# Prompt attention with full-row key products and one value group for each query block

## The chip, the cores and the metric

The kernel runs on one core of one Trainium2 chip. The metric is the device time of one execution in microseconds. Three runs of the kernel before took 994.25, 989.42 and 985.31 us; their median is 989.42 us.

## What is computed

The reference is one inference step of a decoder layer for 512 prompt tokens and 8 sampled sequences of 4 tokens each (544 columns in all, width 1024). One normalised input is projected once; three mixers take their parts of it, and a merge and an output projection end the step. The part around which the change lies is the prompt's attention: 8 query heads in 2 groups of 4, head size 64, with a compressed, a selected and a window branch. For 512 prompt tokens the selected and the window branch see all earlier keys.

```python
h = rmsnorm(x, norm_g) @ w_in                     # one projection, columns split over the mixers
# attention, for each group g, head r of the group, query block of 128
p_c = masked_softmax(q . kcmp + bias)             # 31 compressed keys
p_s = masked_softmax(q . k_sel + bias, causal)    # branch 1
p_w = masked_softmax(q . k_win + bias, causal)    # branch 2
o   = gate0 * p_c @ vcmp + gate1 * p_s @ v_sel + gate2 * p_w @ v_win
# mLSTM (4 heads x 128, chunks) and gated DeltaNet (4 heads x 128, 8 chunks of 64, state S)
o_g: A = tril(kb k^T) ; u, w = (I + A)^-1 [v b, kb e^G] ; S <- S e^GL + k^T (u - w S)
# merge: x + sum_i(sigmoid(merge_i) * ((o_i * silu(z_i)) @ w_branch_i)) @ w_out
```

All of it is float32 to the reference's accuracy, so that a product of two operands is made from an upper and a lower part of each (`wh`, `wl`, `xh`, `xl`): three products instead of one.

## The kernel before

**Order of the work.** The program is traced in Python and a scheduler then writes, for each engine, one fixed list of instructions, by priority and by the times that it expects. Most of TensorE's work are projections: `gemm_steps` (L400 to L410, the products are L407) makes a tile of 128 outputs from 24 products for each half of the 544 tokens, 128x272 each. Tiles of the mixers' gates and of the merge wait in `queue`; `low()` and `fill(n)` (L584 to L599) put them in the list at a low priority, so that they stand between the steps of a chain that has to wait. Each tile of weights is loaded by the SP queue (L390), split by ScalarE (L393) and by VectorE or GpSimd (L396). All engines, and the SP queue's loads and stores too, run their lists in order.

**Places.** Nearly all buffers are ranges of one big tile, `arena`; `Reg(n)` hands out the first free range of n columns, `free()` gives it back, and two further tiles are lent to it while their places are free (`low2`, `low3`). A range that is handed out again waits for the last reader of what lay there.

**Prompt attention** (`att`, L1261 to L1304; head r = 0 is traced ahead of the mLSTM, heads 1 to 3 after it). For a head of both groups, it walks through 4 query blocks i of 128; w = 128 (i + 1) keys are in reach. For each branch b and group g: the scores are an upper product over 128 rows (L1278: both parts of the query against the key's upper part) and a lower product over 64 rows (L1280: the query's upper part against the key's lower part), 128 x w. VectorE adds the bias and takes the maximum (L1285), ScalarE the exponential (L1288), VectorE normalises and gates (L1290), TensorE transposes in pieces of 128 (L351), VectorE or ScalarE copy to a ring `ptr2`. The value products (L1300) add into `acc`, group 0 to its rows 0 to 63 and group 1 to 64 to 127: output tiles of 64 columns of the array. The compressed branch's product comes first (L1272), over 32 rows. The lower parts of the keys of both groups share one slot of `kst`, group 0 on rows 0 to 63 and group 1 on rows 64 to 127 (L1216).

**DeltaNet.** The samples' part loads 8 states of 4 heads (L1570, `Sg`, 4096 columns), forms their outputs (L1597 to L1624), updates them in 8 steps (product L1629, VectorE L1632) and stores them in two halves (L1633). The prompt's part builds decay tables (L1673: `Dm`, `bb`), `Db`, the matrix B (L1689, L1691), inverts its blocks through DRAM (L1712 store, L1714 eight loads back, L1724 and L1726 a chain of small steps on VectorE, L1728 stores, L1729 load back, L1731), composes the inverse (L1742) and then walks through 8 chunks: products L1774, L1785, L1792, L1805 with VectorE and ScalarE between them (L1777, L1787, L1799). A head norm follows chunks 3 and 7 (L1312 to L1316, transposes L351). Then come merge and output, with L1899 and L407.

Of the kernel before, what the change touches and what calls it, by code (L numbers as in the profile page):

```python
# [32 lines left out]
AC = 24932  # L33
A1 = 1280
A2 = 3072
# [55 lines left out]
def _consts():  # L91
# [26 lines left out]
    # one row for each norm, in each group of 32: row t * 2 + g is column 14 of a slice that starts at 14 - 2 t  # L118
# [54 lines left out]
def _layout(i):  # L173
# [33 lines left out]
    # (position of a pair, feature), (tap, pair of positions), group  # L207
# [36 lines left out]
def tile_step(ctx: ExitStack, tc: tile.TileContext, A, O):  # L244
# [20 lines left out]
    # two more tiles, while their places are free: columns 0 to A1 and A1 + 1 to A1 + 1 + A2, the arena's after those  # L265
# [13 lines left out]
    class Reg:  # L279
        """A range of the arena's columns, handed out from its start."""  # L280
# [118 lines left out]
    def gemm_steps(wt, mh, ml, k, sink, rot=0):  # L399
        # the two halves of the tokens, in steps of 8 products  # L400
# [31 lines left out]
    # products of zeros raise the tensor engine's clock while x comes  # L432
# [36 lines left out]
    def norm(k):  # L469
        # the split of the normalised x, for all later projections  # L470
# [6 lines left out]
    # page ids: a row for the registers, and rows of the pools seen as [page, 8 blocks, NQ] for the indirect loads  # L477
# [25 lines left out]
    # gates of the samples' rows (b, g, t, r), two sets of four samples  # L503
# [34 lines left out]
    def silu2(j):  # L538
        # twice silu of a projected tile
# [30 lines left out]
    # outputs of the three branches, feature-major  # L570
# [4 lines left out]
    def prime():  # L575
        # the next tile, its weights on their way
        if queue:
            name, f, t = queue.pop(0)
            g = f(t)
            next(g)  # L580
            job.append((name, g))

    def fill(n):
        # steps of projections that wait for nothing, put between the steps of a chain  # L584
# [8 lines left out]
    @contextmanager  # L593
    def low(n=LOW):
        # work for the gaps of all that is traced later
        p = tc.cur_priority
        tc.cur_priority = p + n
        yield
        tc.cur_priority = p  # L599
# [41 lines left out]
    # m at the start and the end of each chunk: 4 prompt chunks, 8 samples  # L641
# [32 lines left out]
    # DeltaNet gates  # L674
# [11 lines left out]
    # relayout through DRAM: rows c, M, inter, e^-m, ws, NG, e^G, kd, beta  # L686
# [7 lines left out]
    # decays of the chunks on all partitions  # L694
# [12 lines left out]
    # token-major copies  # L707
# [28 lines left out]
    def sums(ps, lhsT, sq, s, first, last):  # L736
        # the sums of a tile's squares over its features, each quarter of the tokens on 32 rows
# [35 lines left out]
    NA = Reg(6 * N + 2 * 5 * 128 + 128 + 32 + 128 + 128)  # L773
# [3 lines left out]
    def rsq(ps, scale, bias, v):  # L777
        # (ss * scale + bias) ** -0.5, in two float32r parts
# [8 lines left out]
    def spread(p, lt, h):  # L787
        # the rows of half the tokens, on all partitions
# [18 lines left out]
    # token-major values of the selected and window branches; window keys of the samples  # L807
# [41 lines left out]
    # in two parts: the rows that they take are of ones and zeros  # L849
# [25 lines left out]
    kc, kx, vc4 = NA.t(32), NA.t(128), NA.t(128)  # L875
    Gh = lambda g: slice(g * 64, g * 64 + 64)
    for i, n in enumerate(('wk', 'wv')):
        nc.sync.dma_start(out=wkv[i], in_=A[n])
    nc.gpsimd.memset(vc4, 0.0)
    nc.gpsimd.memset(kc[:, 31:32], 0.0)  # L880
    # keys and values of both groups, each on its 32 rows
# [6 lines left out]
    for g in range(2):  # L888
        nc.vector.tensor_copy(out=kx[:31, Gh(g)], in_=p[g * 32:g * 32 + 31, :64])
        for r in range(4):  # L890
            (nc.vector.tensor_copy if r % 2 else nc.scalar.copy)(out=vc4[r * 32:r * 32 + 31, Gh(g)],
# [1049 lines left out]
```

## Time and profile before

| what | value |
|---|---|
| median of three runs | 989.42 us |
| profiled execution, span | 989.2 us |
| TensorE busy | 960.3 us (97%) |
| VectorE busy | 518.3 us (52%) |
| ScalarE busy | 350.8 us (35%) |
| GpSimd busy | 304.7 us (31%) |
| value products L1300 | 320 records, 36.9 us busy |
| projections L407, three forms of 1328 | 219.3, 216.0 and 215.1 us busy |

The span runs from the first to the last instruction of one profiled execution; no other time is given for that execution, so the span stands for its time, and it lies 0.2 us under the median of the runs. The busy time of matmuls overlaps, since one starts while the one before it still runs: what a matmul costs is read from the distance of its start to the next start. A float32 matmul (not the `fp32r` kind) leaves two records, so that a value product of one group and one key block is "x2" in the timeline.

### The profile page before, as it was taken

The numbers are of one execution on the slowest core, as the hardware profiler recorded it, in microseconds if no ns is written. First come the engines' busy times: TensorE is split into PE (matmuls) and PEld (weight loads), VectorE is DVE, ScalarE is ACT, GpSimd is POOL, SyncE is SP. The second block draws the span as 40 slices with busy tenths as digits, with TensorE's granted clock in tenths as the row PEclk, the third lists the DMA queues.
The fourth block names the chain that finished last, engine by engine and source line by source line (L and its number), as shares of the span: only waits on it lengthen the run. The fifth ranks groups of instructions, "written<-read, shape, count | busy, mean of one in ns | idle before, by whom it ended". The sixth has DMA issues, their size and how long they took to land.

```text
span 989.2 us, 22049 instructions
## 1 busy us (share of the span) xinstructions
PE 960.3 (97%) x8845; PEld 821.3 (83%) x8845; DVE 518.3 (52%) x1272; ACT 350.8 (35%) x708; POOL 304.7 (31%) x363
## 2 busy tenths in 40 slices
PE   8999998999999999999999999999999899999998
PEld 7888887876878878988878878776987789889998
DVE  6795621520325222666544788777656435756632
ACT  4433353322333432433433355456322222322410
POOL 3122614460054501221232512011261113239610
PEclk7999999999999999999999999999999999999999
DMA  5123858577776788764435223122624712445642
GB/s 219 59 93 98 304 202 277 194 262 238 253 258 215 219 281 276 221 199 119 131 120 176 81 85 107 38 61 84 188 79 135 254 55 67 157 131 166 196 165 69
DMA packets 104424, 161.54 MB, mean 163 GB/s; under 512 B 16949, under 2 KB 65334, under 8 KB 103938
## 3 DMA queue, kind: packets, MB, share of 16 engines
q1 hardware_dynamic: 83946, 121.96, 38.6%
q0 software_dynamic: 6752, 22.19, 6.5%
q10 hardware_dynamic: 13624, 15.98, 4.7%
q8 instruction: 70, 1.15, 0.5%
q14 instruction: 32, 0.26, 0.1%
HBM read 134.86 MB, written 33.10 MB: 170 GB/s over the span
## 4 chain that ended last, share of the span: by engine, by line
PE 78%; DMA 8%; DVE 7%; POOL 2%; issue 2%; SPq 1%; ACT 0%; ACTq 0%; POOLq 0%; DVEq 0%
PE pj L407 49%; PE pacc L1300 3%; PE pa L351 3%; PE pg L351 2%; PE pa L1280 2%; PE pa L1085 2%; DMA arena<-zd 2%; DMA arena<-md 2%; PE pa L1278 1%; PE cacc L967 1%; PE pa L455 1%; PE pg L1445 1%; DMA arena<-in_ps_dram 1%; POOL low L954 1%; PE pa L1774 1%
## 5 line engine op out<-in xcount | busy, mean ns | idle before, releaser
L407 PE MATMUL pj<-xl,wh 128*128 128x272 f32 x1328 | 219.3, 294 | 0.4 <-POOL xl L1839 0.2
L407 PE MATMUL pj<-xh,wl 128*128 128x272 f32 x1328 | 216.0, 293 | 0.6 <-POOL wl L396 0.6
L407 PE MATMUL pj<-xh,wh 128*128 128x272 f32 x1328 | 215.1, 294 | 1.2 <-DVE low L1887 0.4
L407 PEld LDWEIGHTS pj<-xl,wh 128*128 128x128 f32 x1328 | 183.3, 189 | 19.4 <-issue 17.2
L407 PEld LDWEIGHTS pj<-xh,wl 128*128 128x128 f32 x1328 | 182.9, 189 | 16.4 <-issue 14.5
L407 PEld LDWEIGHTS pj<-xh,wh 128*128 128x128 f32 x1328 | 181.8, 189 | 17.2 <-issue 11.6
L393 ACT CAST wh<-wr 128x1024 fp32r<-128x1024 f32 (+1 forms) x107 | 101.6, 951 | 171.0 <-PE pj L407 144.4
L396 POOL TENSOR_TENSOR wl<-wr,wh 128x1024 fp32r<-128x1024 f32 (+1 forms) x34 | 73.4, 2159 | 211.8 <-ACT wh L393 127.4
L396 DVE TENSOR_TENSOR wl<-wr,wh 128x1024 fp32r<-128x1024 f32 (+1 forms) x73 | 85.5, 1171 | 61.5 <-ACT wh L393 44.8
L1288 ACT ACTIVATE arena<-arena 128x128 f32<-128x128 f32 (+3 forms) x64 | 35.6, 557 | 23.6 <-DVE arena L1287 21.7
L954 POOL DMA_INDIRECT low<-in_kc_dram,idxi x32 | 30.7, 959 | 35.0 <-PE pa L351 20.8
L1285 DVE CUSTOM_DVE_ANT_0 arena<-pa,arena 128x128 f32<-128x128 f32 (+3 forms) x64 | 30.8, 486 | 20.2 <-PE pg L351 10.9
L954 POOL DMA_INDIRECT low<-in_vc_dram,idxi x32 | 31.5, 985 | 32.1 <-PE pa L1050 18.8
L1300 PE MATMUL pacc<-arena 128*64 128x128 f32 x320 | 36.9, 286 | 0.0
L567 ACT ACTIVATE arena<-pj 128x272 f32<-128x272 f32 x48 | 18.9, 395 | 48.7 <-PE pj L407 48.6
L1507 DVE SCALAR_TENSOR_TENSOR arena<-arena,vec 128x568 f32<-128x568 f32 x36 | 30.1, 837 | 4.4 <-ACT arena L1505 4.2
L407 PE MATMUL pj<-uh,wh 128*128 128x272 f32 x160 | 26.5, 302 | 6.1 <-DVE arena L752 4.7
L351 PE MATMUL pg<-cst,arena 128*128 128x128 f32 x170 | 31.3, 287 | 1.1 <-DVE arena L1287 1.1
L995 DVE COPY arena<-pa 128x512 f32<-128x512 f32 x16 | 11.1, 691 | 39.9 <-PE pa L351 39.9
L1290 DVE TENSOR_SCALAR arena<-arena,gat 128x128 f32<-128x128 f32 (+3 forms) x64 | 30.8, 489 | 0.5
L351 PE MATMUL pa<-cst,arena 128*128 128x128 f32 (+3 forms) x190 | 30.3, 273 | 0.0
L1300 PEld LDWEIGHTS pacc<-arena 128*64 128x64 f32 x320 | 22.2, 136 | 9.4 <-issue 2.7
(487 smaller groups left out, 1466.0 us busy)
## 6 DMA issues: line engine op xcount, KB each, us to landing
wr<-in_wt_dram SPq DMA_DIRECT2D x75, 512.0 KB, 4.8
gq<-in_ps_dram SPq DMA_DIRECT2D x64, 128.0 KB, 3.0
arena<-in_ps_dram SPq DMA_DIRECT2D x64, 128.0 KB, 2.5
mgd<-arena ACTq DMA_DIRECT2D x24, 272.0 KB, 3.7
arena<-mgd SPq DMA_DIRECT2D x24, 272.0 KB, 2.7
wr<-in_wb_dram SPq DMA_DIRECT2D x24, 256.0 KB, 3.0
wr<-in_wo_dram SPq DMA_DIRECT2D x8, 512.0 KB
out_wino_dram<-in_cw_dram SPq DMA_DIRECT2D x8, 508.0 KB, 5.7
```

What stands on the lines that cost most here:

```text
L351: nc.tensor.transpose(out, in_, ident[:k, :k])
L393: nc.scalar.copy(out=wh[:, :k, :], in_=wr[:, :k, :])
L396: e.tensor_tensor(out=wl[:, :k, :], in0=wr[:, :k, :], in1=wh[:, :k, :].bitcast(F32), op=ALU.subtract)
L407: nc.tensor.matmul(p, lhsT=w[:, c, :], rhs=m[:, (c + rot) % 8, s], start=(i == 0), stop=(i == 3 * k - 1))
L954: nc.gpsimd.indirect_dma_start(out=t.rearrange("p s d -> p (s d)"), out_offset=None, in_=A[src], in_offset=bass.IndirectOffsetOnAxis(ap=id ...
L1085: nc.tensor.matmul(pw[b * 32:b * 32 + 32], lhsT=QB[:, S * 4 + b, :], rhs=keys[b], start=True, stop=True)
L1280: nc.tensor.matmul(ps[g][:, :w], lhsT=hl_[Gh(g), g, qs], rhs=kt_[Gh(g), 3 * b - 1, :w], start=False, stop=True)
L1285: nc.vector.tensor_tensor_reduce(out=P_[:, :w], in0=ps[g][:, :w], in1=tb[g][:, 512 - w:], scale=1.0, scalar=-3e38, op0=ALU.add, op1=ALU.ma ...
L1288: nc.scalar.activation(out=P_[:, :w], in_=P_[:, :w], func=AF.Exp, bias=st[:, 1:2], accum_out=st[:, 2:3])
L1290: nc.vector.tensor_scalar(out=P_[:, :w], in0=P_[:, :w], scalar1=st[:, 3:4], scalar2=gat[:, i, (g * 4 + r) * 3 + b:(g * 4 + r) * 3 + b + 1] ...
L1300: nc.tensor.matmul(acc[Gh(g), qs], lhsT=vtm[b][:, k, Gh(g)], rhs=pts[g][:, k, :], start=False, stop=(b == 2 and k == i))
L1507: nc.vector.scalar_tensor_tensor(out=cv[:, :568], in0=rw[:, j:j + 568], scalar=cvw[:, t, j:j + 1], in1=cv[:, :568], op0=ALU.mult, op1=ALU.add)
```

## The change

1. **Lower key parts on full rows.** Each branch and group has a slot of its own for the lower parts, with zeros in the other 64 rows (four memsets on GpSimd more, `kst` with 8 slots instead of 6). The lower score product uses all 128 rows of the array.
2. **Compressed values on full rows.** `vc4` gets a slot of 128 columns for each head, zero outside of the head's 32 rows; the compressed product reads all 128 rows of `ptc`.
3. **One value group.** The value products of a query block stand after both branches, branch 2 before 1, group 1 before 0, and the compressed product ends the sum. The ring of transposed probabilities grows from 4 to 7.
4. **Places.** `NA` grows by 384 columns, `PR` by 1536; the lent tile is 4096 instead of 3072 columns, the arena 23908 instead of 24932. `PR`, `PC` and `NA` are freed right after DeltaNet's convolution, before the samples' part, instead of after it. By the order of the `Reg` calls the samples' states `Sg` then lie on columns of `NA` and `PR`, and `T3`, `T4`, `T5`, `bb` of the prompt's part (W3) lie on the columns of `Sg`; before, these ranges were apart.

```diff
-AC = 24932
+AC = 23908
-A2 = 3072
+A2 = 4096
...
-    NA = Reg(6 * N + 2 * 5 * 128 + 128 + 32 + 128 + 128)
+    NA = Reg(6 * N + 2 * 5 * 128 + 128 + 32 + 128 + 512)
...
-    kc, kx, vc4 = NA.t(32), NA.t(128), NA.t(128)
+    kc, kx, vc4 = NA.t(32), NA.t(128), NA.t(4, 128)
...
-            (nc.vector.tensor_copy if r % 2 else nc.scalar.copy)(out=vc4[r * 32:r * 32 + 31, Gh(g)],
+            (nc.vector.tensor_copy if r % 2 else nc.scalar.copy)(out=vc4[r * 32:r * 32 + 31, r, Gh(g)],
...
-    kt_ = ks_.enter_context(tc.tile_pool(name="kp", bufs=1)).tile([128, 6, 512], R32, tag="kst", name="kst")
+    kt_ = ks_.enter_context(tc.tile_pool(name="kp", bufs=1)).tile([128, 8, 512], R32, tag="kst", name="kst")
+    klo = {}
     for b in (1, 2):
...
         for g in range(2):
-            gh = slice(g * 64, g * 64 + 64)
-            nc.gpsimd.tensor_tensor(out=kt_[gh, 3 * b - 1], in0=kTt[b][gh, :T], in1=kt_[gh, 3 * b - 3 + g].bitcast(F32), op=ALU.subtract)
+            gh, go = slice(g * 64, g * 64 + 64), slice(64 - g * 64, 128 - g * 64)
+            klo[b, g] = kt_[:, 5 + b if g else 3 * b - 1]
+            nc.gpsimd.memset(klo[b, g][go].bitcast(F32), 0.0)
+            nc.gpsimd.tensor_tensor(out=klo[b, g][gh], in0=kTt[b][gh, :T], in1=kt_[gh, 3 * b - 3 + g].bitcast(F32), op=ALU.subtract)
...
-    PR = Reg(4 * 512 + 5 * 512 + 4 * 512 + 2 * 512 + 8 * 8)
+    PR = Reg(4 * 512 + 5 * 512 + 7 * 512 + 2 * 512 + 8 * 8)
...
-            for g in range(2):
-                nc.tensor.matmul(acc[Gh(g), qs], lhsT=vc4[r * 32:r * 32 + 32, Gh(g)], rhs=ptc[g][r * 32:r * 32 + 32, qs],
-                                 start=True, stop=False)
+            pts = {}
             for b in (1, 2):
-                pts = []
                 ps = [pat() for g in range(2)]
...
-                    nc.tensor.matmul(ps[g][:, :w], lhsT=hl_[Gh(g), g, qs], rhs=kt_[Gh(g), 3 * b - 1, :w], start=False, stop=True)
+                    nc.tensor.matmul(ps[g][:, :w], lhsT=hl_[:, g, qs], rhs=klo[b, g][:, :w], start=False, stop=True)
...
-                    pts.append(pt_)
+                    pts[b, g] = pt_
+
+            for b in (2, 1):
                 for k in range(i + 1):
-                    for g in range(2):
-                        nc.tensor.matmul(acc[Gh(g), qs], lhsT=vtm[b][:, k, Gh(g)], rhs=pts[g][:, k, :], start=False,
-                                         stop=(b == 2 and k == i))
+                    for g in (1, 0):
+                        nc.tensor.matmul(acc[Gh(g), qs], lhsT=vtm[b][:, k, Gh(g)], rhs=pts[b, g][:, k, :],
+                                         start=(b == 2 and k == 0), stop=False)
+            for g in (1, 0):
+                nc.tensor.matmul(acc[Gh(g), qs], lhsT=vc4[:, r, Gh(g)], rhs=ptc[g][:, qs], start=False, stop=True)
...
     LG.free()
     ks_.close()
+    PR.free()
+    PC.free()
+    NA.free()
...
-    # ---- gated DeltaNet, prompt: packs of (head of a pair, 64 positions) on partitions, (pair, chunk) free ----
-    PR.free()
-    PC.free()
-    NA.free()
     YA = Reg(8 * N, True)
```

The scheduler writes new lists for all engines. Lines move by some numbers: scores L1278 and L1280 become L1280 and L1282, value products L1300 become L1304, the compressed product L1272 becomes L1307, and lines behind L1600 move by 6 to 9. Both kernels have 7063 matmuls.

**TensorE in the attention.** First the list of before, around the end of a query block of head 1 (names with `pa` are score banks, `pacc` is the output's bank, `pg` a bank of transposes, `pj` one of a projection).

```order
L1278 MATMUL pa_6243<-kst,hl 128x128
L1280 MATMUL pa_6243<-kst,hl 128x128
L407 MATMUL pj_7381<-xl,wh_7280 128x272
L407 MATMUL pj_7381<-xh,wl_7281 128x272 x7
L351 MATMUL pg_6168<-cst,arena 128x128
L1300 MATMUL pacc_5976<-arena 64x128 x6
L1272 MATMUL pacc_5976<-low,arena 64x128 x2
L351 MATMUL pg_6168<-cst,arena 128x128 x3
```

Now the same kind of place in the changed list, at the end of a block's second branch.

```order
L407 MATMUL pj_7430<-xh,wl_7356 128x272 x2
L1280 MATMUL pa_6187<-kst,hl 128x512
L1282 MATMUL pa_6187<-kst,hl 128x512
L407 MATMUL pj_7430<-xh,wl_7356 128x272 x3
L407 MATMUL pj_7456<-xh,wh_7355 128x272 x8
L407 MATMUL pj_7456<-xl,wh_7355 128x272 x4
L1304 MATMUL pacc_5980<-arena 64x128 x8
L1307 MATMUL pacc_5980<-low,arena 64x128 x2
```

The 160 value products stand in 61 runs before and 17 now; a block's products are 4, 8, 12 or 16 in one run, with the compressed pair behind them.

**SP's queue at the start of the prompt's DeltaNet.** Before, the tables and the block store stand ahead of the samples' stores (L1633 comes later in this list); in brackets is what an entry waits for.

```order
L1570 DMA arena<-in_gS_dram 128x8x128 [waits DVE_49]
L1673 DMA arena<-gs 64x2x512 [waits DMAHW1_49,PE_49]
L1665 DMA arena<-od 128x544 [waits DMAHW2_49,PE_49]
L1673 DMA arena<-gs 64x2x512 [waits DMAHW3_49]
```

Now the tables of `bb` (L1679) stand behind the samples' stores (L1642), and the eight loads L1720 behind the tables.

```order
L1642 DMA out_gSs_dram<-arena 128x16x128 [waits DMAHW3_49,DVE_49]
L1642 DMA out_gSs_dram<-arena 128x16x128 [waits DVE_49]
L390 DMA wr_8815<-in_wt_dram 128x1024 [waits DMAHW5_49,DMAHW0_49,DVE_49]
L1718 DMA bd<-low_7842 128x1024 [waits DVE_49]
L1679 DMA arena<-gs 64x2x512 [waits DMAHW4_49,PE_49]
L1679 DMA arena<-gs 64x2x512
```

**TensorE at the end of the chunk loop.** Before, projections stand between the chunks' products up to the last chunk.

```order
L1774 MATMUL pa_9632<-arena,gq 64x128 x7
L407 MATMUL pj_9896<-xh,wl_9879 128x272 x2
L407 MATMUL pj_9917<-xh,wh_9913 128x272 x4
L407 MATMUL pj_9917<-xl,wh_9913 128x272 x4
L407 MATMUL pj_9917<-xh,wl_9914 128x272 x4
L1785 MATMUL pa_9645<-arena 64x128 x4
L407 MATMUL pj_9931<-xh,wh_9913 128x272 x4
```

Now chunks 5, 6 and 7 follow one another with nothing between them, and the last norm's transposes (L351) follow those.

```order
L1780 MATMUL pa_9636<-arena,gq 64x128 x8
L1791 MATMUL pa_9649<-arena 64x128 x4
L1798 MATMUL pg_9655<-arena 128x128
L1798 MATMUL pg_9656<-arena 128x128
L1798 MATMUL pg_9655<-arena 128x128
L1798 MATMUL pg_9656<-arena 128x128
L1811 MATMUL pa_9665<-arena,low_7842 64x128 x4
L351 MATMUL pa_9676<-cst,arena 128x128 x4
L351 MATMUL pa_9688<-cst,arena 128x128 x4
```

The projections that stood there have moved ahead: between the samples' last product L1638 and the first L1748 of the changed list stand 290 products L407.

## Rows read from the trace of the kernel before

**Rows 1.** The page, part 1: busy us, share of the span, instructions.
```profile
PE 960.3 (97%) x8845; PEld 821.3 (83%) x8845; DVE 518.3 (52%) x1272; ACT 350.8 (35%) x708; POOL 304.7 (31%) x363
```

**Rows 2.** The page, part 4: the chain that ended last, by engine.
```profile
PE 78%; DMA 8%; DVE 7%; POOL 2%; issue 2%; SPq 1%; ACT 0%; ACTq 0%; POOLq 0%; DVEq 0%
```

**Rows 3.** Windows: stretch, length; busy PE, PEld, DVE, ACT, POOL; PEclk; DMA share; GB/s.
```profile
550.00:700.00 150.00, 150.00 (x1081) 114.97 (x1081) 113.06 (x342) 82.00 (x194) 28.75 (x51) 1.00 0.29 89
...
750.00:800.00 50.00, 46.63 (x608) 38.76 (x607) 24.87 (x41) 11.53 (x20) 6.37 (x5) 1.00 0.57 184
```

**Rows 4.** Timeline of TensorE, score products: start, length, engine, line, tiles, count.
```profile
601.69 0.33 PE L1280 MATMUL pa<-kst,hl 64*128 64x128 f32 x2
601.95 0.66 PE L351 MATMUL pg<-cst,arena 128*128 128x128 f32 x4
...
630.14 0.39 PE L1278 MATMUL pa<-kst,hl 128*128 128x512 f32 x1
630.46 0.50 PE L1280 MATMUL pa<-kst,hl 64*128 64x512 f32 x1
630.88 1.13 PE L407 MATMUL pj<-xh,wh 128*128 128x272 f32 x7
...
644.19 0.22 PE L1278 MATMUL pa<-kst,hl 128*128 128x128 f32 x1
644.34 0.32 PE L1280 MATMUL pa<-kst,hl 64*128 64x128 f32 x1
```

**Rows 5.** Timeline of TensorE, value and compressed products.
```profile
644.59 0.87 PE L1300 MATMUL pacc<-arena 128*64 128x128 f32 x10
645.39 0.43 PE L1272 MATMUL pacc<-low,arena 32*64 32x128 f32 x4
645.76 0.65 PE L351 MATMUL pg<-cst,arena 128*128 128x128 f32 x4
...
691.78 1.04 PE L407 MATMUL pj<-xl,wh 128*128 128x272 f32 x7
692.75 0.43 PE L1300 MATMUL pacc<-arena 128*64 128x128 f32 x2
693.11 0.39 PE L407 MATMUL pj<-xl,wh 128*128 128x272 f32 x1
```

**Rows 6.** Waits in the stretch 745 to 800: us in total, times, longest.
```profile
DVE arena L1666 <- DMA arena<-zd: 7.7, 4, 2.8
```

**Rows 7.** Timeline of SP and VectorE, the inverse of the diagonal blocks.
```profile
731.83 3.77 SPq L1714 DMA_DIRECT2D low<-bd  x8
...
757.42 7.35 SPq L1728 DMA_DIRECT2D bd<-low  x8
...
770.27 1.23 DVE L1731 TENSOR_TENSOR arena<-low,cst 128x1024 f32<-128x1024 f32 x1 [1.84 <-DMA low<-bd]
```

**Rows 8.** DMA issues: KB each, median us from issue to landing.
```profile
wr<-in_wt_dram SPq DMA_DIRECT2D x75, 512.0 KB, 4.8
```

**Rows 9.** Timeline of four engines, last chunk and last head norm.
```profile
881.71 0.37 ACT L1787 COPY arena<-pa 128x256 f32<-128x256 f32 x1 [3.12 <-PE pa L1785]
...
885.33 0.65 PE L1805 MATMUL pa<-arena,low 64*64 64x128 f32 x8
885.43 1.12 DVE L1799 SCALAR_TENSOR_TENSOR arena<-arena,bcol,pg 128x128 f32<-128x128 f32 x4 [1.58 <-PE pg L1792]
...
887.79 2.50 POOL L1312 TENSOR_TENSOR arena<-arena 128x512 f32<-128x512 f32 x2
...
894.67 0.66 PE L407 MATMUL pj<-xh,wl 128*128 128x272 f32 x4
895.17 0.60 PE L351 MATMUL pa<-cst,arena 128*128 128x128 f32 x4
```

**Rows 10.** Windows around TensorE's stutter near 849 us.
```profile
847.00:850.00 3.00, 2.27 (x13) 1.13 (x9) 3.00 (x4) 2.12 (x5) 2.44 (x2) 1.00 0.23 87
...
852.00:854.00 2.00, 2.00 (x10) 1.94 (x9) 1.04 (x4) 0.00 (x0) 0.60 (x1) 0.50 0.76 257
```

More of the change, by code (lines that the diff above doesn't have):

```diff
@@ L1249, in tile_step @@
     PS.free()
-    PR = Reg(4 * 512 + 5 * 512 + 4 * 512 + 2 * 512 + 8 * 8)
+    PR = Reg(4 * 512 + 5 * 512 + 7 * 512 + 2 * 512 + 8 * 8)
     osr_ = PR.ring(2, 512)
-    tr_, pr2, ptr2, s8r = PR.ring(4, 512), PR.ring(5, 512), PR.ring(4, 4, 128), PR.ring(8, 8)
+    tr_, pr2, ptr2, s8r = PR.ring(4, 512), PR.ring(5, 512), PR.ring(7, 4, 128), PR.ring(8, 8)
     def qsplit(r):
```

## The prediction

> **What bounds the kernel now.** I read the page's busy times first: TensorE is busy for 960.3 of 989.2 us [rows 1]. Then the chain that ended last: 78% of it is TensorE, 8% transfers, 7% VectorE [rows 2]. So a microsecond of TensorE's time is worth one, as long as nothing else becomes late. The windows say where that could happen [rows 3]: between 550 and 700, where heads 1 to 3 of the attention lie, TensorE has no gap, and VectorE is busy for 113.06 of 150 us; from 750 to 800, in the DeltaNet, TensorE stands still for 3.4 us. Last I read TensorE's timeline, by distances from start to start: four projections L407 take 0.50 us [rows 9], 0.125 each; seven of them ahead of a value product take 0.97 [rows 5], 0.095 more than 7 x 0.125. That 0.095 is the price of going over to a narrower tile.
>
> The sum is made against the span of the profiled execution, 989.2 us, which is 0.2 under the median of the three runs.
>
> **Scores.** A pair of an upper and a lower product, 512 wide, takes 0.32 + 0.42 = 0.74 us [rows 4]; 128 wide it takes 0.15 + 0.25 = 0.40 [rows 4, 5]. A full product behind a full one has a row in L407: by columns 512 cost 0.235 and 128 cost 0.06, but the upper product of 128 shows 0.15 with the change of tile in it, so I take 0.14. New pairs: 0.47 and 0.28, which saves 0.27 and 0.12, for 64 pairs 12.5 by the mean of the two. Where two lower products stand side by side, though, both together take 0.26 [rows 4], no more than one: six places are of that kind, and 12 of the 64 pairs there save 0.05 only. Lower end: 52 x 0.195 + 12 x 0.05 = 11. Upper end: all pairs save what the widest do, 64 x 0.27 = 17. I take **-15**: of the four widths only 128 is held up by more than its columns, so the middle two are nearer to 0.27.
>
> The Trainium skill has a rule against this edit: "TensorEngine Tiling (Array Packing)", section "Key Properties", says that different tiles load weights and multiply in parallel, so that a 64-row product would leave half of the array to another one. The trace agrees where two halves meet (0.26 us for both), but 46 of the 64 pairs stand alone, with a full product behind them, and there the row has 0.42 for one half. By the rule for all pairs this term would be about -2.
>
> **Value products.** Ten records take 0.80 us and two take 0.36 [rows 5]: 0.11 for each further product, 0.22 for a pair of groups. The compressed pair takes 0.37 [rows 5], since it is 32 rows high and starts a mode of its own. The timeline has 64 runs of these two lines. Without a compressed pair there are 31 of 2 records (0.36), 4 of 6 (0.58), 4 of 10 (0.80), 7 of 14 and one of 16 (1.02): 24.9 us. With one behind (0.37 more) there are 5 of 2, one of 4, 4 of 6, 3 of 10 and one of 12: 12.9. Three are compressed alone: 1.1. That is 38.9. With 64 entries at 0.095 it is 45.0. The change makes 16 groups of 2 (i + 1) pairs and a compressed pair of the same tile: 0.37 + 0.22 x 2 (i + 1), so 0.81, 1.25, 1.69 and 2.13, four of each: 23.5. 17 entries add 1.6, one group that is split 0.4: 25.5. **-19.5**; the ends are -13.4 (if the entries were in the 38.9 already) and -21.
>
> **Other changes of tile.** The order of transposes and small products around it has a few islands less: **-1** (0 to -2). TensorE's work falls by **35.5**, between 24 and 40.
>
> **Edits that cost nothing.** Four memsets on GpSimd: the nearest row is a product of 128x512, 1.25 us each [rows 9], so 5 us at most, on an engine that is busy for 31% [rows 1] and long before the first scores. The ring of 7 holds a block's four pieces and three of the next; the fourth waits until the group is done, which TensorE's list puts ahead of it. Without that cover 16 waits of some 0.2 us, 3 in all. The zero rows add no instruction elsewhere.
>
> **What is late next.**
>
> (a) Heads 1 to 3. Three quarters of 35 us leave the 150 us stretch, about 26, so TensorE needs 124 and VectorE still 113, in chains of bias, exponential, normalising and copy. At 91% on VectorE some of its waits come through: **+7**, from 0 to 15.
>
> (b) DeltaNet's places. `Sg` lies on the attention's columns, so its last slice is loaded only after the last value product: 4.8 us for 512 KB [rows 8], beside the projections that stand there; 0 to 5, I take 0. `Db` and `bb` lie on `Sg`: `bb` waits until the second store has left, and since SP works in order, the eight loads L1720, the weights behind them and the whole inverse wait too. From the last product of the samples' update: store about 6 (1 MB, between 4.8 and twice that), the tables' two issues 1.5, from the first of the eight loads to the inverse's end 25.6 (731.83 to 757.42 [rows 7]; 3.77 of it are the loads), then to 770.27 another 12.85 with a wait for transfers in it, of which I take 9, and 1.23 for L1731: 43, at most 53. The cover are 290 projections, 36.3 us, and transposes and products of 4: 40. So **+3**, from -5 to +13. On the other side the four waits for `zd`, 7.7 us on VectorE [rows 6], are gone, since these loads come early now; they stand in the stretch with TensorE's 3.4 us gap: **-3**.
>
> (c) The end of the chunk loop. Before, the last chunk and its norm lie under projections: from 885.33 to 895.17 TensorE never waits [rows 9]. Now chunks 5, 6 and 7 and the norm have nothing between them. For a chunk the copy of 0.37, the state update of 1.12 [rows 9] less the products L1805 of 0.58, a subtraction and the hand-overs stay open: about 2 us, and with parts of the first and last 4.5 for the three. The norm: 9.8 us lie between the last chunk's L1805 and the transposes; GpSimd's squares alone are 2.50 [rows 9]; without the fill that engine and VectorE do nothing else, so 8.5. TensorE's clock: after a stretch of 3 us with 2.27 busy the granted clock stood at 0.50, its 1.2 GHz level, from 852 to 854 [rows 10]. Here such stretches come several times: 2 more. **+15**, from 10 to 20.
>
> The sum: 989.2 - 35.5 + 7 + 3 - 3 + 15 = 975.7, so **976**.
>
> **The rivals.**
>
> 1. *The saving comes through whole.* VectorE keeps up, and the store is quick: -35.5 and -3, and of the tail 5 only: 956. For it: TensorE is the chain's 78%. Against it: the list of TensorE has no fill in the tail. 0.12.
>
> 2. *A new bound eats it.* VectorE sets the pace of heads 1 to 3 (+15), the chain is 8 over its cover, the tail costs 20: 989.2 - 35.5 + 15 + 8 - 3 + 20 = 994 with all at their ends, 985 with half of them. For it: 113 of 124 us. Against it: VectorE's work there is also projection splits, which need not be on time. 0.26.
>
> 3. *Slower: the samples' store holds SP's queue.* The place is the stretch between the last L1638 and L1748. If store, tables and inverse take 53 us, TensorE waits for 13; the weights behind the store and behind the eight loads come late as well, each with 4.8 us of transfer [rows 8] and its split behind it, and then the fill stands still too, some 20 us for four tiles. 975.7 + 10 + 20 = 1006. It decides once this stretch costs 24 us more than I put down. For it: stores, tables, loads and weights share one queue in order. Against it: the loads of most of the fill stand ahead of the stores. 0.13.
>
> 4. *Half tiles overlap after all.* As in the two lower products above; then scores give 2, and 989 is the time. This is the rule of the page named above; 46 lone pairs speak against it. 0.03.
>
> My forecast has the rest, 0.46, with a range of its own of 965 to 986.
>
> **The numbers.** About 1% is what a measurement of this kernel can tell from no change: 979.5 and 999.3. Under 979.5 lie rival 1 and about 0.31 of my 0.46, with a part of rival 2's lower cases, 0.10: 0.53 and a little more for the other ends, 0.55. Above 999.3 lie rival 3 and a tail of rival 2: 0.15. Between: 0.30. The range must leave out 0.2 at most: half of rival 1 under 956, most of rival 3 above 993. **956 to 993.**
>
> **What would show it.** Lower scores L1282 as tiles of 128*128 with 0.23 to 0.24 from start to next start at 512; groups x16 of L1304 followed by x4 of L1307 without a pause, 2.1 us; TensorE's busy time near 925 to 930. In (a), gaps of TensorE in heads 1 to 3 that end with VectorE, a few us together. In (b), one gap ahead of the first L1748, ended by VectorE's L1737, and SP waiting at L1679 for the store. In (c), gaps between chunks 5, 6 and 7 and one of about 8 us ahead of the last transposes. The prediction is wrong in its first part if TensorE's busy time falls by under 25, and in its second if the gaps add up to less than 10 or more than 40 us over the 28.9 that there were.

## The result and the profile after

The changed kernel takes 976.02 us in the median of four runs (975.28 to 979.59), the kernel before 989.81 in four; the ratio is 0.9875 with a 95% interval of 0.9835 to 0.9915. A second set of four on another chip gave 976.42 and a ratio of 0.9834 (0.9783 to 0.9885). The forecast was 976. The sum came out; not each of its terms did, as the sections below show. All ratios in this document compare runs on one chip and leave out a run that is over 1.5% above the fastest of its kernel, which only one of e7's four was.

First the page of the changed kernel, parts 1 and 4 (busy time by engine, the chain by engine).

```profile
span 973.5 us, 22049 instructions
PE 924.3 (95%) x8845; PEld 818.3 (84%) x8845; DVE 523.0 (54%) x1272; ACT 347.8 (36%) x708; POOL 301.9 (31%) x367
...
PE 70%; DVE 13%; DMA 10%; issue 3%; ACT 2%; POOL 1%; SPq 0%; POOLq 0%; DVEq 0%; ACTq 0%
```

TensorE is busy for 36.0 us less than in [rows 1], and it stands still for 973.5 - 924.3 = 49.2 us instead of 28.9. The difference of the spans, 15.7, is 36.0 less 20.3. In the chain VectorE has 13% where [rows 2] had 7%: most of the new waits are for that engine.

The timeline of TensorE in the changed kernel, scores 512 wide and 128 wide, and the group of a block with four key blocks (columns as in [rows 4]).

```profile
572.81 0.39 PE L1280 MATMUL pa<-kst,hl 128*128 128x512 f32 x1
573.04 0.39 PE L1282 MATMUL pa<-kst,hl 128*128 128x512 f32 x1
573.27 1.03 PE L407 MATMUL pj<-xh,wh 128*128 128x272 f32 x7
...
587.38 0.28 PE L1282 MATMUL pa<-kst,hl 128*128 128x128 f32 x1
587.50 0.27 PE L1280 MATMUL pa<-kst,hl 128*128 128x128 f32 x1
587.61 0.28 PE L1282 MATMUL pa<-kst,hl 128*128 128x128 f32 x1
...
598.09 1.97 PE L1304 MATMUL pacc<-arena 128*64 128x128 f32 x32
599.89 0.39 PE L1307 MATMUL pacc<-low,arena 128*64 128x128 f32 x4
600.21 0.44 PE L351 MATMUL pg<-cst,arena 128*128 128x128 f32 x2
```

A pair at 512 takes 0.23 + 0.23 us where [rows 4] had 0.74, a product of 128 takes 0.11 to 0.12, and the whole group 2.12 us, 2.13 in the forecast. From each start to the next, gaps left out, the two score lines add up to 23.1 us (39.3 before), and the two value lines to 23.7 (38.8).

Now the windows, the first row of the kernel before, the others of the changed kernel; the columns are those of [rows 3]. The DeltaNet lies in 700 to 900 before and in 690 to 900 now; the second stretch has fewer records of TensorE (1863 instead of 1979), since projections have moved out of it.

```profile
700.00:900.00 200.00, 195.76 (x1979) 172.00 (x1979) 116.38 (x266) 48.65 (x94) 63.87 (x66) 0.99 0.40 126
```

```profile
550.00:690.00 140.00, 136.80 (x1230) 124.13 (x1228) 114.97 (x365) 79.75 (x195) 24.54 (x49) 0.99 0.38 114
...
690.00:870.00 180.00, 166.89 (x1667) 151.24 (x1668) 97.21 (x193) 41.48 (x79) 58.24 (x59) 0.94 0.42 123
870.00:900.00 30.00, 22.54 (x198) 17.91 (x199) 16.52 (x48) 4.57 (x10) 11.68 (x14) 0.89 0.20 63
```

In the heads 1 to 3 TensorE now stands still for 3.2 us, in the DeltaNet up to 870 for 13.1, and in the 30 us of the last chunks and the norm for 7.5. Before, the whole DeltaNet had 4.2. The granted clock tells a second cost: 0.93 over the 210 us (0.94 and 0.89 in the rows), so that some 14 us of them are lost to a lower clock, against 2 of 200 before. Such a loss stands in the busy time where TensorE works in it. It can be taken out by an estimate from the traces: each distance from start to next start, waits left out, times the clock granted in it. These add up to 951.9 us before and 906.9 now (906.9 in e11 too). So at full clock TensorE's work fell by 45.0 us, and a lower clock than before took back 9.0 of them: 36.0 are left in the busy time. Of the 45.0, 16.2 lie in the two score lines, 15.1 in the two value lines and 10.3 in the projections.

What TensorE waited for in the changed kernel, first from 550 to 690, then from 700 to 900 (us in total, times, longest).

```profile
PE pg L351 <- ACT arena L1298: 1.6, 1, 1.6
PE pa L790 <- DVE gq L1558: 0.9, 1, 0.9
PE pacc L1304 <- ACT arena L1298: 0.4, 1, 0.4
```

```profile
PE pa L351 <- DVE arena L1322: 5.0, 1, 5.0
PE pg L1622 <- DVE low L1726: 3.7, 1, 3.7
PE pj L407 <- DVE arena L544: 3.7, 1, 3.7
PE pa L1748 <- ACT arena L1758: 3.5, 2, 3.3
PE pa L1748 <- DVE low L1760: 2.1, 1, 2.1
PE pg L1798 <- ACT arena L1793: 1.5, 3, 0.5
```

Each has its story on another engine; that of L1622 is in the last section. For L407, near 760, VectorE's list has the part of the gate that waits for a transfer and then the first step of the inverse ahead of L544, which frees a projection's bank:

```profile
758.21 0.35 DVE L1714 SCALAR_TENSOR_TENSOR arena<-arena,hns,low 128x128 f32<-128x128 f32 x1 [5.77 <-DMA arena<-zd]
760.03 0.29 DVE L1723 TENSOR_SCALAR low<-low 128x256 f32<-128x256 f32 x1 [1.47 <-DMA low<-bd]
...
760.59 0.43 DVE L544 SCALAR_TENSOR_TENSOR arena<-arena,pj 128x272 f32<-128x272 f32 x1
```

In SP's list both transfers stand behind the samples' states and the tables. Some of SP's waits from 660 to 800:

```profile
SPq L1642 <- DVE arena L1641: 10.5, 2, 9.7
...
SPq L1720 <- DMA arena<-zd: 2.5, 1, 2.5
SPq L1679 <- DMA out_gSs_dram<-arena: 2.3, 1, 2.3
```

The stores L1642 hold the queue for 10.5 us until the states are updated (the stores L1633 before: 4.7), and the tables L1679 hold it for 2.3 more until the second store has left. In e9, where the tables lie elsewhere, TensorE does not wait for L544 in this stretch. For L1748, near 798, VectorE's list has the merge's product ahead of the step that TensorE waits for, and that product waits for a load:

```profile
797.54 0.79 DVE L1871 SCALAR_TENSOR_TENSOR arena<-arena,hns 128x544 f32<-128x544 f32 x1 [3.67 <-DMA arena<-od]
798.24 0.68 DVE L1760 TENSOR_TENSOR low<-low,pa 128x512 f32<-128x512 f32 x1
```

The end of the chunk loop, TensorE of the changed kernel:

```profile
881.36 0.69 PE L1791 MATMUL pa<-arena 64*64 64x128 f32 x8 [0.44 <-DVE arena L1783]
882.58 0.72 PE L1798 MATMUL pg<-arena 64*128 64x128 f32 x8 [0.53 <-ACT arena L1793]
883.22 0.65 PE L1811 MATMUL pa<-arena,low 64*64 64x128 f32 x8
883.80 1.56 PE L1780 MATMUL pa<-arena,gq 128*64 128x128 f32 x16
885.81 0.69 PE L1791 MATMUL pa<-arena 64*64 64x128 f32 x8 [0.44 <-DVE arena L1783]
887.03 0.71 PE L1798 MATMUL pg<-arena 64*128 64x128 f32 x8 [0.53 <-ACT arena L1793]
887.68 0.65 PE L1811 MATMUL pa<-arena,low 64*64 64x128 f32 x8
893.34 2.07 PE L351 MATMUL pa<-cst,arena 128*128 128x128 f32 x8 [5.01 <-DVE arena L1322]
895.44 2.03 PE L407 MATMUL pj<-xh,wh 128*128 128x272 f32 x7
```

A chunk takes 4.45 us, 1.0 of it shown as standing still (0.44 and 0.53); the rest is short products whose modelled ends fill the hand-overs. The norm is one gap of 5.0. The windows around it:

```profile
887.00:893.30 6.30, 1.30 (x16) 0.94 (x16) 3.96 (x10) 0.00 (x0) 3.88 (x4) 0.82 0.15 42
893.30:897.00 3.70, 3.63 (x14) 2.97 (x15) 2.44 (x5) 1.59 (x4) 1.68 (x4) 0.50 0.00 0
```

After the gap the granted clock is 0.50, 1.2 GHz, for the next 3.7 us, in which TensorE is busy again: seven projections take 2.03 us, where the seven at 573.27 above took 1.03.

### The profile page after: what moved, and what is told of

Its sections match the earlier page's. It is cut to its first block, busy times and chain, and to the rows that moved or that the text cites. A ratio compares the mean times of both kernels' runs of the same rounds, so it can differ in the third digit from the quotient of the medians.

```text
span 973.5 us, 22049 instructions
## 1 busy us (share of the span) xinstructions
PE 924.3 (95%) x8845; PEld 818.3 (84%) x8845; DVE 523.0 (54%) x1272; ACT 347.8 (36%) x708; POOL 301.9 (31%) x367
## 4 chain that ended last, share of the span: by engine, by line
PE 70%; DVE 13%; DMA 10%; issue 3%; ACT 2%; POOL 1%; SPq 0%; POOLq 0%; DVEq 0%; ACTq 0%
PE pj L407 46%; PE pa L351 3%; PE pa L1086 2%; PE cacc L968 2%; DMA low<-in_kc_dram,idxi 1%; DMA arena<-zd 1%; DVE arena L1513 1%; DMA low<-in_vc_dram,idxi 1%; DVE arena L1287 1%; PE pg L351 1%; PE pacc L1304 1%; DVE arena L1292 1%; DVE wl L396 1%; PE pg L1451 1%; DMA od<-arena 1%
## 5 line engine op out<-in xcount | busy, mean ns | idle before, releaser
L407 PE MATMUL pj<-xh,wh 128*128 128x272 f32 x1328 | 214.2, 295 | 4.2 <-DVE arena L544 3.7
L407 PE MATMUL pj<-xl,wh 128*128 128x272 f32 x1328 | 216.3, 294 | 0.0
L407 PE MATMUL pj<-xh,wl 128*128 128x272 f32 x1328 | 216.1, 295 | 0.0
L407 PEld LDWEIGHTS pj<-xh,wh 128*128 128x128 f32 x1328 | 183.5, 191 | 21.8 <-issue 12.2
L407 PEld LDWEIGHTS pj<-xh,wl 128*128 128x128 f32 x1328 | 185.9, 192 | 13.2 <-issue 12.5
L407 PEld LDWEIGHTS pj<-xl,wh 128*128 128x128 f32 x1328 | 185.8, 191 | 11.9 <-issue 10.7
L351 PE MATMUL pa<-cst,arena 128*128 128x128 f32 (+3 forms) x190 | 31.0, 280 | 7.1 <-DVE arena L1322 5.0
L1292 DVE TENSOR_SCALAR arena<-arena,gat 128x128 f32<-128x128 f32 (+3 forms) x64 | 34.1, 537 | 0.7
L351 PE MATMUL pg<-cst,arena 128*128 128x128 f32 x170 | 28.4, 278 | 3.3 <-ACT arena L1298 1.6
L407 PE MATMUL pj<-uh,wh 128*128 128x272 f32 x160 | 25.7, 295 | 6.2 <-DVE arena L752 4.7
L1087 DVE CUSTOM_DVE_ANT_0 arena<-pa,arena 128x512 f32<-128x512 f32 x10 | 6.9, 692 | 44.7 <-PE pa L1086 44.7
L1858 POOL TENSOR_TENSOR arena<-arena 128x272 f32<-128x272 f32 x30 | 26.7, 898 | 12.5 <-DVE arena L1856 12.2
```

The lines of the kernel that those rows point to most:

```text
L351: nc.tensor.transpose(out, in_, ident[:k, :k])
L407: nc.tensor.matmul(p, lhsT=w[:, c, :], rhs=m[:, (c + rot) % 8, s], start=(i == 0), stop=(i == 3 * k - 1))
L1292: nc.vector.tensor_scalar(out=P_[:, :w], in0=P_[:, :w], scalar1=st[:, 3:4], scalar2=gat[:, i, (g * 4 + r) * 3 + b:(g * 4 + r) * 3 + b + 1] ...
L1858: e.tensor_tensor(out=yacc[:, j, s], in0=yacc[:, j, s], in1=tm[:, s], op=ALU.add)
```

## The experiments

All of them stand in one table; "before" is the kernel before on the same chip, and the clock is the mean granted clock of the profiled run.

| run | median us | ratio to before, 95% | span | TensorE busy | still | clock |
|---|---|---|---|---|---|---|
| changed | 976.02 | 0.9875 (0.9835 to 0.9915) | 973.5 | 924.3 | 49.2 | 0.979 |
| e1 places only | 998.01 | 1.0102 (1.0038 to 1.0166) | 997.6 | 962.9 | 34.7 | 0.988 |
| e2 e1 + lower parts | 993.78 | 1.0017 (0.9983 to 1.0052) | 996.1 | 953.7 | 42.4 | 0.973 |
| e3 e1 + value group | 996.65 | 1.0094 (1.0049 to 1.0139) | 995.8 | 945.0 | 50.8 | 0.978 |
| e4 changed, states at the end | 954.01 | 0.9621 (0.9578 to 0.9665) | 957.6 | 920.7 | 36.9 | 0.987 |
| e5 e1, states at the end | 986.06 | 0.9992 (0.9949 to 1.0034) | 980.9 | 951.4 | 29.5 | 0.994 |
| e6 e2, states at the end | 973.22 | 0.9829 (0.9765 to 0.9892) | 973.0 | 942.5 | 30.5 | 0.989 |
| e7 e3, states at the end | 983.18 | 0.9893 (0.9810 to 0.9975) | 987.2 | 946.9 | 40.3 | 0.977 |
| e8 e4, compressed on 32 rows | 964.33 | 0.9752 (0.9697 to 0.9806) | 956.6 | 921.8 | 34.8 | 0.989 |
| e9 changed, VP on the states | 967.30 | 0.9761 (0.9701 to 0.9820) | 963.9 | 921.3 | 42.6 | 0.986 |
| e10 e4, copies on ScalarE | 965.67 | 0.9716 (0.9657 to 0.9776) | 964.8 | 923.0 | 41.8 | 0.982 |
| e11 changed again | 976.42 | 0.9834 (0.9783 to 0.9885) | 974.3 | 926.2 | 48.1 | 0.977 |

**e1, the places alone.** The kernel before, with the regions freed where the change frees them:

```diff
+    PR.free()
+    PC.free()
+    NA.free()
     lend(B2, pool("lp2", 1).tile([128, A2], F32, tag="low3", name="low3"), A2)
...
-    PR.free()
-    PC.free()
-    NA.free()
     YA = Reg(8 * N, True)
```

> The kernel before with one edit: PR, PC and NA are freed ahead of DeltaNet's samples' part, so that the samples' states lie on the attention's columns and W3 on theirs. Theory (the places cost, the tile edits gain): TensorE's busy time stays at 960 +- 4 us, waits appear in the DeltaNet and at the last norm, which has 13 projections behind the last chunk instead of 73; span 4 to 12 us longer, 993 to 1001. Rival (the new place is harmless or even lets loads start earlier): 985 to 991, no new gap of TensorE over 2 us behind 690.

It took 998.01 us, 1.0% longer, as the theory had it. TensorE's busy time is where it was, and 13 projections stand behind the last chunk. Its waits between 400 and 960 begin with the last norm, as expected, and a projection's bank, which was not named ahead:

```profile
PE pa L351 <- DVE arena L1316: 5.7, 1, 5.7
PE pj L407 <- DVE arena L544: 4.9, 2, 3.7
```

**e2, lower parts of the keys on full rows, the value products as before.**

```diff
 # on e1; AC, A2 and kst as in the change
+            klo[b, g] = kt_[:, 5 + b if g else 3 * b - 1]
+            nc.gpsimd.memset(klo[b, g][go].bitcast(F32), 0.0)
...
-lhsT=hl_[Gh(g), g, qs], rhs=kt_[Gh(g), 3 * b - 1, :w]
+lhsT=hl_[:, g, qs], rhs=klo[b, g][:, :w]
```

> The kernel before with the early places and the lower key parts on full rows; value products as before. Theory: both score lines together take 23 us from start to next start instead of 39; value and compressed products stay at 38 to 39; the time is that of the places alone less 14 to 17 us. Rival (two halves of the array overlap in most pairs, so full rows save little): less 2 to 4 us.

The score lines take 25.3 us instead of 40.8 in e1, 15.5 less where 16 were expected. The time fell by 4.2 by the medians and by 0.85%, some 8 us, by the ratios, not by 14 to 17. Its ten runs lie apart: four from 986.3 to 988.1 with a clock of 0.984 to 0.988, six from 992.4 to 998.9 with 0.973 to 0.981. The page, of one of the six, says where the rest is there: TensorE stands still for 7.7 us more than in e1, and its clock is 0.973 instead of 0.988. So the time came out between the theory and the rival, and the product as in the theory: much of the saving was made and spent in the DeltaNet, whose last two chunks follow each other without a projection.

**e3, the value group alone, with the compressed values on full rows.**

```diff
 # on the changed kernel; AC, A2 and kst as before
-            klo[b, g] = kt_[:, 5 + b if g else 3 * b - 1]
-            nc.gpsimd.memset(klo[b, g][go].bitcast(F32), 0.0)
...
-lhsT=hl_[:, g, qs], rhs=klo[b, g][:, :w]
+lhsT=hl_[Gh(g), g, qs], rhs=kt_[Gh(g), 3 * b - 1, :w]
```

> The kernel before with the early places, the value group with branch 2 first and the compressed values on full rows; lower key parts in 64 rows as before. Theory: value and compressed products take 24 us from start to next start instead of 39, and some 40 entries into a narrow tile go, so that the time is that of the places alone less 17 to 20 us. Rival (the products only move, a group waits for its last piece): less 5 to 10 us, with gaps of TensorE ahead of the groups that end with VectorE or ScalarE.

The value lines take 23.7 us instead of 37.8 in e1, and TensorE's busy time fell by 17.9, but the time by 1.4, less than either side had. It stands still for 50.8 us, 16 more than e1, at the places that the changed kernel shows (L351 5.0, L407 3.9, L1622 3.7, L1748 3.3 and 2.2), and not ahead of the value groups, where the rival put it. With both edits together the time falls by 22 against e1, and the changed kernel stands still no longer than e3. These numbers fit a cost of the uncovered DeltaNet that is paid once, by the first edit that shortens the attention, so that a second comes through whole; no run separates that from other changes of the lists.

**e4, the states somewhere else.** One word in the changed kernel:

```diff
-    SG = Reg(4096 + 1024 + 9 * 128 + 64 * 2 + 16)
+    SG = Reg(4096 + 1024 + 9 * 128 + 64 * 2 + 16, True)
```

> The changed kernel with one edit: the region of the samples' states is taken from the end of the free columns, so that W3 of the prompt's part no longer lies on it. Theory (waits of the places cost what the gaps behind 690 show: 3.7 + 3.7 + 5.6 and 7.4 us of standing still, against 4.2 before, and about 13 us of lower clock with them): 12 to 20 us less than the changed kernel, 956 to 964. Rival (the stalls are the order of VectorE and of the merge's loads and only move on): 972 to 978, TensorE's idle time stays near 49 us.

954.01 us: 2 us below the theory's stretch, far from the rival, and the fastest of all. `True` takes the region from the end of the free columns, where the prompt's tables do not lie. The word moves two things, though: the tables leave the states, and the states leave the columns of `NA` (a part of their region, 2572 columns, still lies on `PR`). The list of TensorE then has 73 projections behind the last chunk again, as before the change, where the changed kernel has none. They had been drawn ahead: between the last L1638 and the first L1748 the changed kernel has 290, e4 has 25, and the kernel before had 28. Its windows and the last chunk's and the norm's rows:

```profile
690.00:880.00 190.00, 184.48 (x1854) 163.21 (x1844) 110.70 (x243) 48.92 (x93) 71.96 (x69) 1.00 0.42 128
```

```profile
853.59 0.65 PE L1811 MATMUL pa<-arena,low 64*64 64x128 f32 x8
...
863.43 0.60 PE L351 MATMUL pa<-cst,arena 128*128 128x128 f32 x4
```

5.5 us of standing still where the changed kernel has 20.6, at clock 1.00 instead of 0.93. The norm still takes 9.8 us from L1811 to its transposes; it is under projections. The profile is of the longest of e4's four runs. Of the waits listed above, 2.2 us ahead of L1748 are still there.

**e5, e6, e7: the three kernels e1, e2 and e3 with the states at the end**, by the same word.

```diff
-    SG = Reg(4096 + 1024 + 9 * 128 + 64 * 2 + 16)
+    SG = Reg(4096 + 1024 + 9 * 128 + 64 * 2 + 16, True)
```

> The kernel of the places alone (e1) with the samples' states at the end of the free columns, no edit of the attention. Theory (the overlap of W3 with the states is what the places cost): 986 to 993, the kernel before within 0.4%, projections again between all chunks. Rival (the early freeing costs by itself): 995 to 1001. Rival (the end of the free columns is a gain by itself, and would explain much of the 22 us of e4): 965 to 975.

> Lower key parts on full rows alone, with the states at the end. Theory (a saved microsecond of TensorE is a saved microsecond while projections cover the DeltaNet's waits): e5 less 14 to 17 us, 970 to 976; score lines 23 to 25 us from start to next start. Rival (what e2 showed, 4 us, is what full rows are worth): 983 to 988.

> Value group and compressed values on full rows alone, with the states at the end. Theory: e5 less 17 to 20 us, 967 to 973; value lines 24 us from start to next start. Rival (what e3 showed, 1 us, is what the group is worth): 985 to 990.

e5 is the kernel before, within its interval: neither the early freeing nor the end of the free columns is worth more than the half per cent that these runs can tell. e6 took 12.8 us less than e5 by the medians and 1.6%, 16 us, by the ratios, where the theory had 14 to 17, with the score lines at 25.1 us. e7 is a miss in part: by the ratio it is 1.0% under e5, some 10 us, where 17 to 20 were expected and about 1 by the rival; its interval reaches from 2 to 18. Its value lines take 23.4 us as they should (38.5 in e5), but its profile stands still for 10.8 us more than e5's (3.7 at L1746, 2.7 and 2.6 at projections). That profile is of the longest of its runs, 989.0 us where the shortest took 971.2, so these waits need not be those of the others, and what holds e7's time up stays open. At full clock, by the estimate above, TensorE's work is 947.7 us in e5, 932.5 in e6, 925.7 in e7 and 908.5 in e4: 15 for one edit, 22 for the other, 39 for both. Together the two edits give e4, 32 us under e5 by the medians of two chips.

**e8, the compressed product in 32 rows again**, on e4, still behind the group. `vc4` has one slot again, so `NA` is 384 columns narrower and what follows it lies elsewhere.

```diff
-lhsT=vc4[:, r, Gh(g)], rhs=ptc[g][:, qs]
+lhsT=vc4[r * 32:r * 32 + 32, Gh(g)], rhs=ptc[g][r * 32:r * 32 + 32, qs]
```

> The changed kernel with the states at the end (e4), but the compressed values in the head's 32 rows, still behind the value group. Theory (a change of tile height costs some 0.1 us, and the pair 0.37 instead of 0.22 to 0.33): e4 plus 1 to 4 us, 955 to 958, the 16 compressed pairs at 0.37 us each plus an entry. Rival (full rows for the compressed product carry a large part of the gain): 960 to 966.

The compressed line takes 5.8 us, 0.37 for each pair. e4's 5.5 and its value lines hold 1.7 us of lower clock; at full clock both lines take 25.7 us here and 23.7 in e4, and all of TensorE's work 911.7 and 908.5: 3 more, inside the theory's 1 to 4. The median, 964.33, is 10 over e4's, on another chip; by the ratios it is 1.3%, 13 us, and their intervals (0.9578 to 0.9665, 0.9697 to 0.9806) do not meet. So the time is the rival's and the products are the theory's. The two profiles can't settle it, since their spans are 956.6 and 957.6: e8's is of its shortest run and e4's of its longest. This stays open.

**e9, another buffer on the states' columns.**

```diff
+    VP = Reg(2048 * 2 + 1024 + 1024 + 64)
     W2, W3 = Reg(2 * 1024), Reg(4 * 1024)
...
-    VP = Reg(2048 * 2 + 1024 + 1024 + 64)
```

> The changed kernel, the samples' states where it has them, but VP (values, keys and state of the chunks) is handed out ahead of W2 and W3, so that VP lies on the states' columns and the tables Db and bb do not. Theory (what hurts is that the inverse's first inputs wait for the samples' stores, not that something does): 36 projections stand behind the last chunk instead of none, no wait for the store ahead of the inverse; 955 to 966. Rival (any buffer of the prompt's DeltaNet on the states holds the chain as long): 972 to 980.

967.30 us, 9 less than the changed kernel on that chip and a little over the theory's end. What lies on the states matters: with values and keys there instead of `Db` and `bb`, 36 projections stand behind the last chunk, and the waits ahead of the norm's transposes are 2.5 and 1.4 us instead of 5.0 in one. SP no longer waits at L1679 for the store, as expected. 165 projections stand between the last L1638 and the first L1748, between e4's 25 and the changed kernel's 290. But this is 9 of e4's 22 us; what the other 13 are for is not separated. One thing that e9 keeps and e4 has lost is the wait at L1622, 4.0 us here.

**e10, all copies of the transposed probabilities on ScalarE**, on e4.

```diff
-                    (nc.scalar.copy if g else nc.vector.tensor_copy)(out=pt_[:, :i + 1], ...
+                    nc.scalar.copy(out=pt_[:, :i + 1], ...
```

> The kernel of e4 with the copies of all transposed probabilities on ScalarE; before, VectorE made half of them. Theory (in heads 1 to 3 VectorE at 44 of 50 us is what TensorE waits for): VectorE's busy time between 550 and 690 falls by some 10 us, TensorE's idle time there from 6 us to 2 or 3, the time by 2 to 4 us against e4, 950 to 953. Rival (ScalarE, busy for 36 of 50 us there, becomes the one that is late, or the waits are those of a chain): the same idle time or more, 954 to 960.

The theory fell. The median, 965.67, lies above both stretches; by the ratios it is 1.0% over e4, with intervals that just meet, and the two ran on different chips: no gain is seen, and whether it is a loss is not settled. From 550 to 690, e4 and then e10:

```profile
550.00:690.00 140.00, 133.99 (x1244) 121.33 (x1246) 113.53 (x365) 78.72 (x194) 26.27 (x49) 0.99 0.36 109
```

```profile
550.00:690.00 140.00, 133.21 (x1187) 120.80 (x1185) 102.48 (x329) 86.10 (x219) 29.17 (x48) 1.00 0.37 111
```

VectorE has 11 us less to do, and TensorE stands still for 6.8 instead of 6.0. So in e4 VectorE's load in the heads is not what holds TensorE there; the waits are single ones (3.7 us at L1609 in e4, 5.4 at L1594 in e10).

**e11, the changed kernel again.**

> The changed kernel again, beside the two others on one chip. Both theories: 973 to 980.

976.42, as expected; the waits of its profile are those shown above, to 1.2 us each.

## Why the prediction was right

The profile's 15.7 us, by the forecast's own terms, with TensorE's work at full clock by the estimate above:

| term | forecast | measured |
|---|---|---|
| TensorE's work | -35.5 | -45.0 |
| lower clock in that work | +2 | +9.0 |
| (a) standing still, heads 1 to 3 | +7 | +3.2 |
| (b) standing still, DeltaNet up to 870 | +3 - 3 | +8.9 |
| (c) standing still, last chunks and norm | +13 | +7.5 |
| standing still elsewhere | 0 | +0.7 |
| sum | -13.5 | -15.7 |

Of the terms, only the scores came close by themselves. The sum held because the errors have both signs, and that part is luck.

**Scores, -15:** measured -16.2 from start to next start. The count by pairs held. The runs agree with the rows, in e2, e6 and the changed kernel alike. The Trainium skill ("TensorEngine Tiling (Array Packing)", section "Key Properties") says that different tiles can load weights and multiply in parallel, by which the term would have been about -2. The trace agrees with that for the few pairs side by side only.

**Value products, -19.5:** the lines gave 15.1. The entries, 4.5 by the forecast, stand in the products ahead of them, and can be read there: a projection ahead of a value product takes 0.216 us to the next start in the median, where it takes 0.125 ahead of another projection. There were 42 such places before and 12 are left, which is 2.7 us.

**TensorE's work, -35.5:** 36.0 by the busy time, but that agreement is made of two errors, 9.5 more work saved and 7 more of lower clock. One price was put at nothing: coming back from the narrow tile. The first projection behind a lower score product took 0.230 us in 37 places before and takes 0.126 in 33 now, which is 3.9 us; seven projections are 1.13 us long behind such a product in [rows 4], and 1.03 at 573.27 above. With the 2.7 this explains 6.6 of the 10.3 that the projections gave; the rest stays open.

**(a) Heads 1 to 3, +7:** 3.2 us between 550 and 690. The term was too large, and its mechanism did not hold: of the 2.9 us listed above, 2.0 end with ScalarE's copies L1298, not with VectorE, and e10, on e4, took 11 us of work from VectorE without a gain.

**(b) DeltaNet's places, +3 and -3:** the step that was wrong. It expected one gap ahead of the first L1748, with SP at the store. SP did wait at L1679 for the store (2.3 us) and at the stores for 10.5, but TensorE reached L1748 without a gap, behind the 290 projections, and stood still at four other places, for 13.1 us up to 870, where the whole stretch had 4.2 before: +9 instead of 0. Three of them are VectorE's or ScalarE's lists, in which a step that waits for a late transfer stands ahead of the one that TensorE needs: the forecast looked for the wait where the data is used, and it came out where the engines' lists were blocked. The fourth, at L1622, stands behind an operation of VectorE that ends with GpSimd's (last section).

**(c) The end of the loop, +15:** the place is right, the size was 7.5 of standing still, where 13 were put down, since the norm took 5.0 and not 8.5 when GpSimd and VectorE have nothing else to do, and a chunk shows 1.0. The clock was put at 2; it cost 12.5 us of the busy time in the DeltaNet (0.06 of 166.89 and 0.11 of 22.54), and 9.0 more over the whole kernel than before.

**Rival 3**, the store that holds SP's queue, has its mechanism in the trace, at a smaller price: e9 takes it away, and 9 us with it. e4 takes away 22, for more reasons than this one.

## What to carry to other kernels

On an engine that is busy for 97%, products in a narrow tile cost their own time, some 0.1 us for going into the other tile and as much for coming back, and a full tile with zeros in half of its rows is cheaper, unless the other half is at work just then. An edit that saves memory or time in one place changes what a list can cover in another: look for the first stretch in which the fill runs out, and for buffers handed out over one whose store must leave first. Where two edits give little alone and much together, a fixed stall may be in between, and one word on where a buffer lies may be worth more than the edit.

## What the runs showed of the hardware

On two of the three chips the time of the kernel before goes with its mean granted clock, run by run: spans from 981.5 us at 0.998 to 994.5 at 0.983 in 17 runs, and from 980.6 at 0.997 to 993.5 at 0.979 in 13. Among seven runs on the third chip it does not (992.2 at 0.993, 991.3 at 0.983). The product of span and clock differs less than the span, but it is no constant: e7's four runs have spans of 969.5 to 987.2 and products of 960.1 to 968.3. Seventeen runs of the kernel before have a median product of 978, the changed kernel's eight are between 949 and 954, e4's four between 939 and 945. The changed kernel pays for its gaps twice, by the gaps and by a clock of 0.972 to 0.979, where the kernel before ran at 0.979 to 0.998 beside the experiments.

One operation of VectorE, 128 x 128, took 6.47 us in both profiles of the changed kernel and in e3 and 6.72 in e9, 0.42 and 0.71 in the kernel before and e4; TensorE's wait at L1622 (3.7 us) stands behind it. GpSimd works beside it on the states' decay, L1640, without a pause:

```profile
694.43 6.47 DVE L1617 TENSOR_SCALAR arena<-arena,gSr 128x128 f32<-128x128 f32 x1
696.79 4.02 POOL L1640 TENSOR_TENSOR arena<-arena,bcol 128x512 f32<-128x512 f32 x4
...
701.04 0.65 PE L1622 MATMUL pg<-arena 32*32 32x128 f32 x8 [3.71 <-DVE low L1726]
```

VectorE's operation ends at 700.89, 0.08 us behind GpSimd's series at 700.81. The same holds in nine of the thirteen profiles, whatever it took there (0.71 to 6.72 us): it ends 0.08 to 0.09 us behind the end of one of GpSimd's products. In the other four it started just as GpSimd went over to the memset L1724, and took 0.41 to 0.45. The operation just ahead of it, L1616, which reads a bank of TensorE's output, took 0.34 beside the same series. By these coincidences GpSimd's products held it back; no run moved them, so this is not tested.
